# The five slots of the weight ring begin at five different distances from the moving tiles

## The chip, the cores and the metric

The kernel runs on one core of a Trainium2 chip. The metric is the device time of one execution in microseconds. Three runs of the kernel before took 790.16, 791.92 and 792.40 us; the median is 791.92 us.

## The reference, cut to what matters

One layer of a hybrid encoder block over 512 tokens of width 1024: a token mixer, a cross-attention into 256 memory tokens, and a SwiGLU feed-forward. All of it is float32. The change touches the feed-forward alone:

```python
def swiglu(h, w_gate_up, w_down):
    g, u = jnp.split(h @ w_gate_up, 2, axis=-1)
    return (jax.nn.silu(g) * u) @ w_down
...
        h = rms_norm(x, g_ffn_pre[l])
        x = x + rms_norm(swiglu(h, w_gate_up[l], w_down[l]), g_ffn_post[l])
```

`w_gate_up` is 1024 x 5632, `w_down` is 2816 x 1024.

## The kernel before, in words

Each float32 product is made from three matmuls (`mm3`, lines 139 to 142): every operand is split into a rounded part `hi` and a rest `lo`, and hi*hi, hi*lo and lo*hi are added up in PSUM. Line 140 loads the stationary hi and streams the moving hi, line 141 loads the same stationary hi again and streams the moving lo, line 142 loads the stationary lo and streams the moving hi. So every matmul has a weight load of 128 x 128 of its own, which runs beside the matmul before it: while TensorE streams one moving tile out of SBUF, it also reads the next stationary tile out of SBUF.

The gate and up projections after the first block run in units. Most units (`seven`, line 1077) use a Strassen-like scheme: 7 products of 12 matmuls with 256 columns each instead of 8. A few (`eight`, line 1040; blocks 2, 3 and 11) make all 8. There are 17 seven-units and 3 eight-units. The moving operands are the normalised activations `b1`, `b2` and sums of them, `thi` and `tlo`. The stationary operand is always a weight block out of a ring.

The ring is a pair of tiles, `ring_hi` and `ring_lo`, of 4160 float32 elements per partition (lines 869 and 870). Five slots stand in it: two single ones of 512 elements (one product each) and three double ones of 1024 elements (two products each, or half an eight-unit). `single()` and `double()` give the place at which a slot begins, in elements of 4 bytes, each in turn. A seven-unit takes one single slot and three double ones, an eight-unit two double ones. A slot is filled by a DMA into `raw`, for some of them sums on VectorE (lines 929 to 932), a cast on ScalarE into `ring_hi` (line 902) and a subtraction on VectorE into `ring_lo` (line 903). `take` fills a slot as soon as the items that overlap its place have been taken for use.

The compiled program puts `b1`, `b2`, the `t` tiles, `ring_hi` and `ring_lo` at addresses that are multiples of 256 bytes, and all steps inside them (256 or 128 elements) are multiples of 512 bytes. So the distance from the moving operand to the stationary one, modulo 256 bytes, is that of the slot alone. Before, `AS_WEIGHTS` is 16 elements: every slot begins at 64 bytes modulo 256.

After the gate and up blocks, the same ring holds `w_down` in four slots at 0, 1024, 2048 and 3072 elements (line 953). There the ring is the moving operand, in tiles of 512 columns. These four places stay as they are, and each overlaps the same old slots before and after.

Earlier stages hold other distances. In the first projection (lines 291 to 300) `hTh` and `hTl` are stationary, at multiples of 512 bytes, and `vhi`, `vlo` are moving. For the tile of 256 columns the distance is 0. For the tile of 264 columns block k begins at k times 1056 bytes, so the distance of stationary from moving is 192 bytes for k = 2, 160 for k = 3, 128 for k = 4, 96 for k = 5 and 64 for k = 6.

Of the kernel before, what the change touches and what calls it, by code (L numbers as in the profile page):

```python
# [32 lines left out]
AS_WEIGHTS, AS_MOVING = 16, 48  # L33
# [3 lines left out]
def hybrid_block_kernel(  # L37
# [606 lines left out]
    with tc.tile_pool(name="cross", bufs=1, reuse_waits="tile") as cp:  # L644
# [221 lines left out]

        ring_hi = cp.tile([P, 4160], F32R, tag="kT", name="ring_hi")
        ring_lo = cp.tile([P, 4160], F32R, tag="hh", name="ring_lo")  # L870
        sums = big.tile([P, 2, 4, 4, P], F32, tag="sB", name="sums")
# [36 lines left out]
        nslot = [0, 0]  # L908

        def single():  # L910
            nslot[0] += 1
            return AS_WEIGHTS + 512 * (nslot[0] % 2)

        def double():
            nslot[1] += 1
            return AS_WEIGHTS + 1024 + 1024 * (nslot[1] % 3)

        def seven_weights(n, c0):
            raw, total = {}, sums[:, n % 2]
            s2, s4, s3, s1 = (total[:, i] for i in range(4))  # L920

            def a11():
                raw["lower"] = load_raw(w_gate_up, 0, 4, c0, 256)
                raw["upper"] = load_raw(w_gate_up, 4, 4, c0, 256)
                return raw["lower"][:, :, :P]

            def s2_s4():
                lower, upper = raw["lower"], raw["upper"]
                dve.tensor_tensor(out=s1, in0=lower[:, :, P:], in1=upper[:, :, P:], op=ALU.add)
                dve.tensor_tensor(out=s2, in0=s1, in1=lower[:, :, :P], op=ALU.add)  # L930
                dve.tensor_tensor(out=s4, in0=s2, in1=upper[:, :, :P], op=ALU.add)
                dve.tensor_tensor(out=s3, in0=lower[:, :, :P], in1=lower[:, :, P:], op=ALU.add)
                return total[:, 0:2]

            two = dict(c=2, k=4, n=P)
            item(at := single(), 512, fill_from(at, dict(k=4, n=P), a11))
            item(at := double(), 1024, fill_from(at, two, s2_s4))
            item(at := double(), 1024, fill_from(at, two, lambda: raw["upper"], "p c k n -> p k c n"))
            item(at := double(), 1024, fill_from(at, two, lambda: total[:, 2:4]))
# [301 lines left out]
```

## Time and profile before

| | |
|---|---|
| median of three runs | 791.92 us |
| profiled execution, whole | 792.46 us |
| its span, first to last instruction | 790.4 us |
| TensorE busy | 766.5 us, 97% of the span, 4796 matmuls |
| VectorE, ScalarE busy | 554.4 us (70%), 413.6 us (52%) |
| ring stage with 256-column matmuls | about 464 to 663 us of the span |
| `w_down` stage | about 663 to 785 us |

The span is one execution as the profiler saw it; some 2.1 us of the time lie outside it. TensorE's busy time is nearly the span because a matmul counts as busy from its start to its modelled end, so matmuls overlap. How fast TensorE goes is therefore read from the starts: the time from one matmul's start to the next one's, or the number of matmuls in a stretch.

### The profile page before, as it was taken

The numbers are of one execution on the slowest core, as the hardware profiler recorded it, in microseconds if no ns is written. First come the engines' busy times: TensorE is split into PE (matmuls) and PEld (weight loads), VectorE is DVE, ScalarE is ACT, GpSimd is POOL, SyncE is SP. The second block draws the span as 40 slices with busy tenths as digits, with TensorE's granted clock in tenths as the row PEclk, the third lists the DMA queues.
The fourth block names the chain that finished last, engine by engine and source line by source line (L and its number), as shares of the span: only waits on it lengthen the run. The fifth ranks groups of instructions, "written<-read, shape, count | busy, mean of one in ns | idle before, by whom it ended". The sixth has DMA issues, their size and how long they took to land.

```text
span 790.4 us, 12322 instructions
## 1 busy us (share of the span) xinstructions
PE 766.5 (97%) x4796; PEld 674.0 (85%) x4796; DVE 554.4 (70%) x999; ACT 413.6 (52%) x755; POOL 70.6 (9%) x110
## 2 busy tenths in 40 slices
PE   7999999999999999999999999999999999999996
PEld 7887788887778888877778999999999999888885
DVE  6567889879886588545653778998899988414214
ACT  7358888757875457444543635544354448113111
POOL 6001232010321101000002100000000000000001
PEclk9999999999999999999999999999999999999998
DMA  6342112421322725411350212232433333423302
GB/s 243 84 130 57 52 55 75 138 72 64 107 80 96 282 77 187 131 56 54 134 160 0 81 49 86 81 108 82 148 99 107 103 107 114 152 80 107 106 2 107
DMA packets 60745, 80.01 MB, mean 101 GB/s; under 512 B 2704, under 2 KB 43664, under 8 KB 60688
## 3 DMA queue, kind: packets, MB, share of 16 engines
q1 hardware_dynamic: 59264, 74.49, 29.1%
q0 software_dynamic: 1280, 4.72, 1.8%
q8 instruction: 38, 0.62, 0.3%
q14 instruction: 19, 0.16, 0.1%
q10 hardware_dynamic: 144, 0.02, 0.0%
HBM read 77.13 MB, written 2.10 MB: 100 GB/s over the span
## 4 chain that ended last, share of the span: by engine, by line
PE 72%; DVE 11%; ACT 7%; issue 4%; DMA 3%; POOL 2%; SPq 0%; DVEq 0%; POOLq 0%; ACTq 0%
PE ps_a L141 14%; PE ps_a L140 14%; PE ps_a L142 14%; PE ps_s L140 4%; PE ps_s L142 4%; PE ps_s L141 4%; DVE ring_lo L903 3%; PE ps_t L140 2%; PE ps_t L141 2%; PE ps_t L534 2%; PE ps_t L142 2%; DMA raw<-in_dram 2%; PE ps_o L543 1%; PE ps_s L515 1%; PE ps_o L140 1%
## 5 line engine op out<-in xcount | busy, mean ns | idle before, releaser
L902 ACT CAST ring_hi<-fraw 128x1024 fp32r<-128x1024 f32 (+1 forms) x62 | 57.6, 933 | 102.6 <-PE ps_o L142 37.0
L903 DVE TENSOR_TENSOR ring_lo<-fraw,ring_hi 128x1024 fp32r<-128x1024 f32 (+1 forms) x62 | 66.6, 1076 | 63.2 <-ACT ring_hi L902 63.0
L126 DVE TENSOR_TENSOR lo<-raw,hi 128x1024 fp32r<-128x1024 f32 x56 | 68.2, 1224 | 22.2 <-ACT hi L125 21.9
L142 PE MATMUL ps_a<-hTh,lo 128*128 128x512 f32 x192 | 76.8, 400 | 0.6 <-DVE lo L126 0.6
L141 PE MATMUL ps_a<-hTl,hi 128*128 128x512 f32 x192 | 76.0, 396 | 0.0
L140 PE MATMUL ps_a<-hTh,hi 128*128 128x512 f32 x192 | 75.8, 395 | 0.2 <-ACT hi L125 0.2
L125 ACT CAST hi<-raw 128x1024 fp32r<-128x1024 f32 x56 | 57.8, 1048 | 24.4 <-PE ps_a L141 15.4
L902 ACT CAST ring_hi<-sums 128x1024 fp32r<-128x1024 f32 x34 | 35.7, 1050 | 56.5 <-PE ps_a L141 23.9
L903 DVE TENSOR_TENSOR ring_lo<-sums,ring_hi 128x1024 fp32r<-128x1024 f32 x34 | 41.5, 1222 | 4.3 <-ACT ring_hi L902 4.1
L142 PEld LDWEIGHTS ps_a<-hTh,lo 128*128 128x128 f32 x192 | 36.1, 188 | 7.3 <-DVE lo L126 1.0
L141 PEld LDWEIGHTS ps_a<-hTl,hi 128*128 128x128 f32 x192 | 36.1, 188 | 6.4
L140 PEld LDWEIGHTS ps_a<-hTh,hi 128*128 128x128 f32 x192 | 36.2, 188 | 6.1 <-ACT hi L125 0.4
L529 ACT ACTIVATE p<-p,nm 128x128 f32<-128x128 f32 (+1 forms) x64 | 36.1, 564 | 8.4 <-DVE nm L519 7.6
L140 PE MATMUL ps_a<-b,ring_hi 128*128 128x256 f32 x140 | 39.0, 279 | 0.0
L141 PE MATMUL ps_a<-b,ring_hi 128*128 128x256 f32 x140 | 39.0, 278 | 0.0
L142 PE MATMUL ps_a<-b,ring_lo 128*128 128x256 f32 x140 | 39.0, 278 | 0.0
L140 PE MATMUL ps_s<-b,ring_hi 128*128 128x256 f32 x128 | 35.5, 278 | 0.0
L141 PE MATMUL ps_s<-b,ring_hi 128*128 128x256 f32 x128 | 35.5, 278 | 0.0
L142 PE MATMUL ps_s<-b,ring_lo 128*128 128x256 f32 x128 | 35.5, 278 | 0.0
L536 ACT CAST pth<-ps_t 128x128 fp32r<-128x128 f32 (+1 forms) x64 | 27.1, 425 | 14.5 <-PE ps_t L534 13.7
L537 DVE TENSOR_TENSOR ptl<-ps_t,pth 128x128 fp32r<-128x128 f32 (+1 forms) x64 | 30.7, 487 | 4.9 <-ACT pth L536 3.6
L534 PE MATMUL ps_t<-ident,p 128*128 128x128 f32 x160 | 28.1, 275 | 1.1 <-DVE p L531 0.8
(425 smaller groups left out, 2504.4 us busy)
## 6 DMA issues: line engine op xcount, KB each, us to landing
raw<-in_dram SPq DMA_DIRECT2D x64, 512.0 KB, 3.6
fraw<-in_dram SPq DMA_DIRECT2D x62, 512.0 KB, 3.5
cb<-in_dram SPq DMA_DIRECT2D x8, 256.0 KB, 2.6
xo<-in_dram POOLq DMA_DIRECT2D x4, 512.0 KB, 5.6
out_dram<-yd SPq DMA_DIRECT2D x8, 256.0 KB, 2.0
rawv<-in_dram SPq DMA_DIRECT2D x3, 520.0 KB, 6.1
xt<-in_dram SPq DMA_DIRECT2D x3, 512.0 KB, 6.9
gb<-in_dram POOLq DMA_DIRECT2D x3, 512.0 KB, 5.1
```

The costliest lines, as they stand in the source:

```text
L125: act.copy(hi[:, j : j + n, :], raw)
L126: dve.tensor_tensor(out=lo[:, j : j + n, :], in0=raw, in1=f32(hi[:, j : j + n, :]), op=ALU.subtract)
L140: pe.matmul(dst, sh, mh, start=first, stop=False)
L141: pe.matmul(dst, sh, ml, start=False, stop=False)
L142: pe.matmul(dst, sl, mh, start=False, stop=last)
L515: pe.matmul(s[:, :w], q[:, h, ts], kt[:, h, :w], start=True, stop=False)
L529: act.activation(p[:, :n], p[:, :n], AF.Exp, bias=nm, scale=-1.0, accum_out=sm)
L534: pe.transpose(tp[:, k * P : (k + 1) * P], p[:, k * P : (k + 1) * P], ident)
L536: act.copy(span(ph, i), t3)
L537: dve.tensor_tensor(out=span(pl, i), in0=t3, in1=f32(span(ph, i)), op=ALU.subtract)
L902: act.copy(h2, v)
L903: dve.tensor_tensor(out=l2, in0=v, in1=f32(h2), op=ALU.subtract)
```

## The change

Only the five places change, as multiples of 4 bytes: the two single slots begin at 16 and 536 elements (64 and 96 bytes modulo 256) in place of 16 and 528; the three double ones at 1056, 2088 and 3120 (128, 160 and 192 bytes) in place of 1040, 2064 and 3088. No instruction is added or removed and none is moved; the order on every queue stays.

```diff
         def single():
             nslot[0] += 1
-            return AS_WEIGHTS + 512 * (nslot[0] % 2)
+            return (16, 512 + 24)[nslot[0] % 2]
 
         def double():
             nslot[1] += 1
-            return AS_WEIGHTS + 1024 + 1024 * (nslot[1] % 3)
+            return (1024 + 32, 2048 + 40, 3072 + 48)[nslot[1] % 3]
```

(A blank line is added ahead of line 869, so later lines of the kernel after stand one further down.)

## Rows read from the trace of the kernel before

**Rows 1.** The page: span, busy time, and the span in 40 slices.
```profile
span 790.4 us, 12322 instructions
...
PE 766.5 (97%) x4796; PEld 674.0 (85%) x4796; DVE 554.4 (70%) x999; ACT 413.6 (52%) x755; POOL 70.6 (9%) x110
...
PE   7999999999999999999999999999999999999996
...
PEclk9999999999999999999999999999999999999998
```

**Rows 2.** Busy time by stretch, all engines (us and instructions; clock, DMA share, GB/s).
```profile
core 0: us, PE busy (x) PEld busy (x) DVE busy (x) ACT busy (x) POOL busy (x), PEclk, DMA share, GB/s
454.00:493.00 39.00, 39.00 (x334) 39.00 (x333) 32.54 (x38) 17.15 (x21) 0.00 (x0) 1.00 0.19 59
493.00:603.00 110.00, 107.77 (x939) 106.78 (x939) 101.65 (x146) 52.40 (x79) 0.00 (x0) 1.00 0.35 109
603.00:634.00 31.00, 31.00 (x260) 30.58 (x259) 30.22 (x45) 13.64 (x21) 0.00 (x0) 1.00 0.33 105
634.00:663.00 29.00, 28.61 (x252) 28.42 (x251) 23.73 (x34) 15.85 (x27) 0.00 (x0) 1.00 0.27 92
663.00:785.00 122.00, 121.03 (x540) 100.11 (x538) 44.32 (x57) 30.78 (x44) 2.21 (x4) 1.00 0.27 95
```

**Rows 3.** Matmuls alone, in stretches without a pause.
```profile
core 0: us, PE busy (x), PEclk, DMA share, GB/s
464.00:493.00 29.00, 29.00 (x249) 1.00 0.20 62
555.00:583.00 28.00, 28.00 (x250) 1.00 0.41 127
604.00:613.00 9.00, 9.00 (x79) 1.00 0.30 90
614.00:633.00 19.00, 19.00 (x164) 1.00 0.31 97
634.00:643.00 9.00, 9.00 (x82) 1.00 0.31 105
644.00:662.00 18.00, 18.00 (x161) 1.00 0.25 88
686.00:718.00 32.00, 32.00 (x143) 1.00 0.22 78
```

**Rows 4.** Timeline of TensorE around 607 us, first and thirteenth matmul.
```profile
606.20 0.28 PE L140 MATMUL ps_a<-thi,ring_hi 128*128 128x256 f32 x1
...
607.62 0.28 PE L140 MATMUL ps_a<-b,ring_hi 128*128 128x256 f32 x1
```

**Rows 5.** Timeline of TensorE around 566 us, first and tenth matmul.
```profile
565.87 0.28 PE L140 MATMUL ps_a<-b,ring_hi 128*128 128x256 f32 x1
...
566.89 0.28 PE L140 MATMUL ps_a<-b,ring_hi 128*128 128x256 f32 x1
```

**Rows 6.** What TensorE waited for, 486 to 663 us (total, times, longest).
```profile
PE ps_t L140 <- DVE U L1090: 1.7, 2, 1.3
PE ps_a L140 <- DVE G L1090: 0.8, 3, 0.4
```

**Rows 7.** Timeline, first projection, 256 columns at distance 0, first and twelfth.
```profile
21.40 0.28 PE L140 MATMUL ps_a<-vhi,hTh 128*128 128x256 f32 x1
...
22.72 0.28 PE L142 MATMUL ps_a<-vhi,hTl 128*128 128x256 f32 x1
```

**Rows 8.** Timeline, first projection, 264 columns, first and last for k = 2 to 6.
```profile
12.51 0.28 PE L140 MATMUL ps_s<-vhi,hTh 128*128 128x264 f32 x1
...
13.59 0.28 PE L140 MATMUL ps_a<-vhi,hTh 128*128 128x256 f32 x1
...
15.03 0.28 PE L140 MATMUL ps_s<-vhi,hTh 128*128 128x264 f32 x1
...
16.49 0.28 PE L140 MATMUL ps_a<-vhi,hTh 128*128 128x256 f32 x1
...
20.29 0.29 PE L140 MATMUL ps_s<-vhi,hTh 128*128 128x264 f32 x1
...
21.28 0.29 PE L142 MATMUL ps_o<-vhi,hTl 128*128 128x264 f32 x1
...
22.84 0.29 PE L140 MATMUL ps_s<-vhi,hTh 128*128 128x264 f32 x1
...
24.30 0.28 PE L140 MATMUL ps_a<-vhi,hTh 128*128 128x256 f32 x1
...
29.18 0.29 PE L142 MATMUL ps_s<-vhi,hTl 128*128 128x264 f32 x1
...
30.03 0.28 PE L140 MATMUL ps_a<-vhi,hTh 128*128 128x256 f32 x1
```

**Rows 9.** Instructions that write `ring_hi` and `ring_lo`: ns min/median/max, first and last start.
```profile
L902 ACT CAST ring_hi<-fraw x62: 609/1048/1057, 436.7 to 762.3; 128x1024 fp32r<-128x1024 f32 x45, 128x512 fp32r<-128x512 f32 x17
L903 DVE TENSOR_TENSOR ring_lo<-fraw,ring_hi x62: 683/1220/1228, 437.9 to 763.4; 128x1024 fp32r<-128x1024 f32 x45, 128x512 fp32r<-128x512 f32 x17
```

## The prediction

> **What bounds the kernel now.** First the page: TensorE is busy for 766.5 of 790.4 us and its granted clock stands at 9 tenths or more in every slice but the last [rows 1]. So the end moves by what TensorE's pace moves, wherever TensorE does not wait. Then the stretches: the change acts only where the ring is stationary, about 464 to 663 us. There VectorE is the nearest other engine, 101.65 of 110 us between 493 and 603 us, and 30.22 of 31 us between 603 and 634 us; ScalarE is at half [rows 2]. TensorE's idle time from 493 to 603 us is 110 - 107.77 = 2.2 us, and the waits put it on VectorE's sums of the seven-units: 1.7 us before a product into `ps_t`, 0.8 us before one into `ps_a` [rows 2, 6].
>
> The view that matters is the pace of the matmuls, by count. A matmul lasts 0.28 us and is counted in every window it touches, so the time per matmul is (window + 0.28) / count. It has two values in the ring stage: 28.28 / 250 = 113.1 ns from 555 to 583 us, and 29.28 / 249 = 117.6 ns from 464 to 493 us [rows 3]. The starts say the same: 1.02 us over nine steps, 113.3 ns, around 566 us; 1.42 us over twelve steps, 118.3 ns, around 607 us [rows 4, 5]. I use 113.3 and 117.7. From 634 to 643 us it is 113.2, from 644 to 662 us 113.5, from 604 to 613 us 117.5, from 614 to 633 us 117.6 [rows 3]. So a stretch is wholly fast or wholly slow, and the pace changes at TensorE's pauses, not with the slot, the moving tile or the load of the other engines: the granted clock is 1.00 in both. This looks like two read streams, moving tile and next weights, that fall into step after a pause and stay so, since every matmul repeats the same distance of 64 bytes. This lock is my reading; the rows show the two paces and that they last.
>
> How much is lost to it: the slow stretches run from about 463.7 to 493.3 and from 603.4 to 633.3 us, less some 0.6 us of pauses, so (29.6 + 29.3) us / 117.7 ns = 500 matmuls at 4.4 ns over the fast pace: 2.2 us. All the ring's 256-column matmuls are 17 x 84 + 3 x 96 = 1716 by the code, so 29% are slow.
>
> **The change part by part.** Nothing is added, removed or moved on any queue; no wait is new. Three things could cost or give.
>
> (a) The writes into the ring start at other offsets. The casts and subtractions of `fraw` run both at 64 bytes modulo 256 (gate and up) and at 0 (`w_down`), and the longest is 9 and 8 ns over the median of 1048 and 1220 ns [rows 9]. 17 x 4 + 3 x 2 = 74 slots are filled; 74 x 8 ns = 0.6 us on VectorE is an end upward, as much downward the other. No row has an odd multiple of 32 bytes for these. I take 0; ScalarE, half idle, covers its share, and VectorE's would lie beside TensorE except in the 2.2 us of waits.
>
> (b) The pace at the new distances. Of the 1716 matmuls, 204 use single slots (half stay at 64 bytes, half go to 96) and 1512 use double ones, 504 each at 128, 160 and 192. No row shows 256 columns at these. Bounds: the fast end is 113.3 ns, because the `w_down` stage, where a 512-column matmul gives the weights twice the time, goes at 32.39 us / 143 = 226.5 ns, the same per column [rows 3]; the stream itself seems to need that. The slow end is distance 0 with 256 columns, 1.32 us / 11 = 120.0 ns [rows 7]. All 1512 at 120.0 cost 10.1 us against all fast, 7.9 us more than the 2.2 us lost today; all fast gains 2.2 us.
>
> Between these ends stand the 264-column rows of the first projection, the only ones at the new distances [rows 8]: at 192 bytes 1.08 us / 9 = 120.0 ns, at 160 1.46 / 12 = 121.7, at 128 0.99 / 8 = 123.8, at 96 1.46 / 12 = 121.7, and at 64 0.85 / 7 = 121.4. These are no prices for 256 columns (at 64 bytes the ring itself has 113.3 or 117.7), so I use only their differences from 64 bytes: +2.4 ns at 128, +0.3 at 160, -1.4 at 192, +0.3 at 96. 504 x (2.4 + 0.3 - 1.4) ns + 102 x 0.3 ns = +0.7 us. Each stretch there has about ten matmuls, so this sum is hardly different from 0; I take 0 and keep the 0.7 for the range.
>
> (c) The lock. A slot is left after 12, 24 or 48 matmuls, and the next one stands at another distance, so the streams are shifted against each other by 32 bytes or more. If each slot then draws anew at today's odds, 29% stay slow, only better mixed: no gain. If a fast stretch survives the shift and a slow one ends with its slot, nearly all 2.2 us come back. No row shows a shift without a pause, so I take the middle, 1.1 us. What is late next is VectorE: in the slow stretch from 603 to 634 us it is busy for 30.22 of 31 us, so at most 0.8 us can be won there [rows 2]; half of that stretch's 1.1 us fits, and none of the gain is hidden.
>
> **Sum.** Profiled execution 792.46 (span 790.4 and 2.1 outside) + 0 + 0 - 1.1 = 791.4 us. That is 0.5 under the median of 791.92; the three runs, 790.16 to 792.40, are just as far apart as the 2.2 us between all fast and today's mix.
>
> At two places the Trainium skill says otherwise. The rows show a pace that differs between distance 0 (120.0 ns) and 64 (113.3 or 117.7) [rows 3, 7]. The page "SBUF — State Buffer", section "Who interferes with whom", gives TensorE two independent read ports for moving operand and weights, and says that TensorE never waits on anyone; by that rule distances would not matter and the time would stay at 792.46 us. The trace speaks against it. And the page "TensorE: Matmul & The Clock Gate", section "Back-to-back issue gap", gives N / 2.4 + 2.5 ns, 109.2 ns for 256 columns, as the gap; no stretch of the ring gets there.
>
> **The rivals.**
>
> *Slower: the new distances lock worse.* The 128-byte slots fall to the pace of distance 0 and the other double ones to the slow pace. For it: 128 bytes is the slowest of the 264-column rows, and no double slot keeps the 64 bytes that have the fast pace [rows 8]. Against: 192 bytes is the fastest of them. Price: 504 x 6.7 + 1008 x 4.4 = 7.8 us, less today's 2.2 = 5.6; TensorE's 2.2 us of waits on VectorE can swallow part, since there a slower TensorE waits less: 3.4 to 5.6, so 795.9 to 798.1 us. It decides from 545 more slow matmuls than today's 500 (2.4 us).
>
> *The change does nothing.* Whatever sets the pace at a pause, hardware other than the distance, holds on through the slots: 792.46 us, or whatever mix of stretches the run draws, 790.2 to 792.5. For it: paces change only at pauses today. Against: distance 0 differs from 64.
>
> *Faster: a third pace.* At some distance the streams never meet, and the matmul goes below 113.3 ns. For a price I take the same step downward as from slow to fast, 4.4 ns, for two of the three double slots: 1008 x 4.4 + 2.2 = 6.6 us, 785.8 us, with VectorE's 92% [rows 2] giving back up to half: 785.8 to 789. Against: 226.5 ns at 512 columns says that 113.3 is the stream's own.
>
> **How the numbers follow.** Less than 0.3%, 2.4 us, can't be told from no change in this kernel. The forecast (locks end sooner; from 790.2, all fast, to 793.2, no gain and the 0.7 of (b)) has 0.50; nothing changes 0.15; locks worse 0.26; a third pace 0.09. The all-fast end of the forecast, 790.2, is within 0.3% of the median, so faster holds the third pace and a little of the forecast: 0.13. Slower is the worse lock and its milder mixes: 0.28. Same is 0.59. The range from 789.3 to 796.6 leaves out most of the third pace and the upper half of the worse lock.
>
> **What would show it.** Right: in the profile after, no stretch of 20 us in the ring stage stands at 117.7 ns throughout; the count per stretch lies between the two paces, and the pace changes at slots. Wrong: one slot with its own pace of 118 ns or more in every unit (worse lock), the paces still changing only at pauses (nothing), or any stretch under 113 ns (third pace). The casts and subtractions into the ring should keep 1048 and 1220 ns; if they lengthen, (a) was mis-sized. What would overturn the forecast most cheaply is the 128-byte slot at 120 ns: 504 x 6.7 = 3.4 us by itself.

## The result, and the profile after

The kernel after takes 794.93 us (median of 20 runs, 793.47 to 796.46), the kernel before 791.86 us (20 runs, 789.21 to 794.77). The ratio is 1.0044, 95% interval 1.0035 to 1.0053: slower by 0.44%. The forecast was 791.4.

The page of the kernel after, its span, busy time and slices, against [rows 1]:

```profile
span 792.6 us, 12322 instructions
...
PE 772.3 (97%) x4796; PEld 680.9 (86%) x4796; DVE 554.1 (70%) x999; ACT 413.3 (52%) x755; POOL 71.5 (9%) x110
...
PE   8999999999999999999999999999999999999996
...
PEclk9999999999999999999999999999999999999998
```

Same instructions, same granted clock; TensorE is busy 5.8 us longer, and the span grew by 2.2. Busy time by stretch, all engines, against [rows 2] (the last stretch begins 2.5 us later, since the ring stage ends later):

```profile
core 0: us, PE busy (x) PEld busy (x) DVE busy (x) ACT busy (x) POOL busy (x), PEclk, DMA share, GB/s
454.00:493.00 39.00, 38.97 (x331) 38.76 (x331) 32.59 (x38) 17.38 (x21) 0.00 (x0) 1.00 0.22 68
493.00:603.00 110.00, 109.30 (x919) 108.56 (x918) 99.64 (x142) 50.85 (x76) 0.00 (x0) 1.00 0.32 102
603.00:634.00 31.00, 30.94 (x264) 30.73 (x264) 30.08 (x44) 13.71 (x20) 0.00 (x0) 1.00 0.33 104
634.00:665.50 31.50, 31.45 (x266) 31.24 (x266) 25.95 (x38) 17.37 (x29) 0.00 (x0) 1.00 0.30 100
665.50:785.00 119.50, 119.50 (x533) 99.16 (x533) 43.33 (x54) 29.34 (x42) 2.21 (x4) 1.00 0.26 93
```

Between 493 and 603 us 919 matmuls stand where 939 stood, although TensorE is idle for 0.7 us in place of 2.2. So each matmul takes longer. The waits of TensorE from 486 to 667 us are down to one, against 1.7 and 0.8 us [rows 6]:

```profile
PE ps_t L140 <- DVE U L1091: 0.6, 1, 0.6
```

Matmuls alone, in stretches without a pause of note, against [rows 3]:

```profile
core 0: us, PE busy (x), PEclk, DMA share, GB/s
464.00:492.00 28.00, 28.00 (x238) 1.00 0.22 66
497.00:511.00 14.00, 14.00 (x120) 1.00 0.23 75
555.00:583.00 28.00, 28.00 (x240) 1.00 0.37 116
636.00:664.00 28.00, 28.00 (x239) 1.00 0.28 95
686.00:718.00 32.00, 32.00 (x143) 1.00 0.24 82
```

With the same reckoning, (window + 0.28) / count: 118.8, 119.0, 117.8 and 118.3 ns in the ring stage. None of these stretches is at 113.3 any more. The `w_down` stage, which the change leaves alone, has the same 143 matmuls in 32 us.

The pace is now that of the slot. The starts of the first matmul of three double slots in a row, 48 matmuls each (blocks 2 and 3, made in full), and of the single slot behind them; then those of two later double slots, 24 apart:

```profile
466.87 0.28 PE L140 MATMUL ps_a<-b,ring_hi 128*128 128x256 f32 x1
...
472.53 0.28 PE L140 MATMUL ps_s<-b,ring_hi 128*128 128x256 f32 x1
...
478.23 0.28 PE L140 MATMUL ps_s<-b,ring_hi 128*128 128x256 f32 x1
...
483.98 0.28 PE L140 MATMUL ps_a<-b,ring_hi 128*128 128x256 f32 x1
...
570.86 0.28 PE L140 MATMUL ps_a<-b,ring_hi 128*128 128x256 f32 x1
...
573.58 0.28 PE L140 MATMUL ps_a<-tlo,ring_hi 128*128 128x256 f32 x1
```

The slot at 192 bytes: 5.66 us / 48 = 117.9 ns. The one at 128: 5.70 / 48 = 118.8. The one at 160: 5.75 / 48 = 119.8. The 192-byte slot again at 570.86: 2.72 / 24 = 113.3. So 192 has the two paces that 64 had, and 128 and 160 are slow each in its own way: in every unit the 128-byte slot took 118.3 to 119.0 ns a step and the 160-byte slot 119.2 to 120.1.

Over the whole ring stage, from all starts in the trace, each slot's mean time from one start to the next (steps over 130 ns, the pauses, left out; before, where all slots stand at 64 bytes, the mean of all):

| slot, distance | matmuls | before, ns | after, ns | added, us |
|---|---|---|---|---|
| single, 64 bytes | 96 | 114.7 | 115.6 | 0.1 |
| single, 96 | 108 | 114.7 | 118.3 | 0.4 |
| double, 128 | 504 | 114.7 | 118.6 | 2.0 |
| double, 160 | 504 | 114.7 | 119.8 | 2.6 |
| double, 192 | 504 | 114.7 | 116.3 | 0.8 |

That is 5.8 us (column added: matmuls times the difference). The time above 113.3 ns in the steps over 130 ns shrank from 4.95 to 2.72 us, so 2.2 us of it went into waits that TensorE had anyway. Left are 3.5 us; the ring stage, from its first to its last matmul (13 early ones, done between those of the first block, left out), grew from 200.20 to 203.61 us, 3.4 us. In the two profiled executions the stages ahead of the ring happened to take 1.2 us less after (463.9 and 462.7 us to its first matmul), which gives the 2.2 us of the spans. The medians are 3.1 us apart.

The writes into the ring kept their durations, against [rows 9]:

```profile
L903 ACT CAST ring_hi<-fraw x62: 611/1048/1057, 435.8 to 764.6; 128x1024 fp32r<-128x1024 f32 x45, 128x512 fp32r<-128x512 f32 x17
L904 DVE TENSOR_TENSOR ring_lo<-fraw,ring_hi x62: 683/1219/1228, 437.0 to 765.6; 128x1024 fp32r<-128x1024 f32 x45, 128x512 fp32r<-128x512 f32 x17
```

### The profile page after: what moved, and what is told of

It reads as the page before. It is cut to its first block, busy times and chain, and to the rows that moved or that the text cites. A ratio compares the mean times of both kernels' runs of the same rounds, so it can differ in the third digit from the quotient of the medians.

```text
span 792.6 us, 12322 instructions
## 1 busy us (share of the span) xinstructions
PE 772.3 (97%) x4796; PEld 680.9 (86%) x4796; DVE 554.1 (70%) x999; ACT 413.3 (52%) x755; POOL 71.5 (9%) x110
## 4 chain that ended last, share of the span: by engine, by line
PE 75%; DVE 9%; ACT 6%; issue 4%; DMA 3%; POOL 2%; SPq 0%; DVEq 0%; POOLq 0%; ACTq 0%
PE ps_a L140 14%; PE ps_a L141 14%; PE ps_a L142 14%; PE ps_s L141 4%; PE ps_s L142 4%; PE ps_s L140 4%; PE ps_t L140 2%; PE ps_t L141 2%; PE ps_t L142 2%; DVE ring_lo L904 2%; PE ps_t L534 2%; DMA raw<-in_dram 2%; PE ps_o L543 1%; PE ps_o L140 1%; PE ps_o L141 1%
```

## The experiments

Three explanations stood against each other. A: each distance between the moving tile and the next weights has paces of its own, and 96, 128 and 160 have bad ones. B: it is the shift at each slot change that costs. C: the offset of a slot by itself is bad, whatever the place of the moving tile. All kernels are the one before with other places in the ring; the diffs show the two lines of `single()` and `double()`.

**All slots at 128.**

```diff
-            return AS_WEIGHTS + 512 * (nslot[0] % 2)
+            return (32, 512 + 32)[nslot[0] % 2]
...
-            return AS_WEIGHTS + 1024 + 1024 * (nslot[1] % 3)
+            return (1024 + 32, 2048 + 32, 3072 + 32)[nslot[1] % 3]
```

> All five slots at 128 bytes modulo 256, so no slot change shifts the distance. Theory A (each distance has its own pace; 128 is one of the bad ones): every ring stretch at 118 to 119 ns per matmul, as in the 128-byte slot of the changed kernel; 1716 x (118.6 - 114.7) = 6.7 us more than before, less 2 to 4 us that the waits on VectorE swallow: 794.5 to 797 us. Theory B (it is the shift at each slot change that costs, whatever the distance): no shifts, so the two paces of before, 113.3 and 117.7 ns, and 790 to 793 us.

Measured 795.07 us (8 runs), ratio 1.0043 [1.0027, 1.0058] to the kernel before.

**All slots at 160.** The same with 40 in place of 32.

> All five slots at 160 bytes modulo 256. Theory A: 119.8 to 120.4 ns throughout, 1716 x 5.3 = 9 us, less 3 to 5 us of waits on VectorE that shrink: 796 to 798.5 us, slower than with all at 128. Theory B: no shifts, 790 to 793 us.

Measured 796.47 us (6 runs), ratio 1.0057 [1.0040, 1.0073].

**All slots at 192.** The same with 48.

> All five slots at 192 bytes modulo 256, which in the changed kernel ran partly at 113.3 and partly at 117.7 ns. Theory A: the same two paces as at 64 bytes, changing at pauses, and 790 to 794 us. Theory B: also as before, 790 to 793 us. A third possibility: 192 was fast only where a 160-byte slot came before it; then it stays at 117.7 throughout, 1716 x 3 = 5 us less waits, 793.5 to 795.5 us.

Measured 793.39 us (12 runs), ratio 1.0014 [1.0002, 1.0026]. The same three stretches of each of these kernels follow, with columns as above; the count of matmuls is the number to read. All slots at 128:

```profile
464.00:484.00 20.00, 20.00 (x171) 1.00 0.26 76
544.00:564.00 20.00, 20.00 (x171) 1.00 0.36 107
647.00:663.00 16.00, 16.00 (x137) 1.00 0.27 92
```

All slots at 160:

```profile
464.00:484.00 20.00, 20.00 (x169) 1.00 0.26 78
544.00:564.00 20.00, 20.00 (x169) 1.00 0.34 106
647.00:663.00 16.00, 16.00 (x136) 1.00 0.23 69
```

All slots at 192:

```profile
464.00:484.00 20.00, 20.00 (x179) 1.00 0.24 66
544.00:564.00 20.00, 20.00 (x172) 1.00 0.41 122
647.00:663.00 16.00, 16.00 (x138) 1.00 0.21 67
```

At 128: 20.28 / 171 = 118.6 ns, then 118.6 and 118.8. At 160: 20.28 / 169 = 120.0, then 120.0 and 119.7. At 192: 113.3 in the first stretch, 117.9 and 118.0 in the others, the two paces of 64 bytes. With no shift at all, 128 and 160 are as slow as in the changed kernel. B as the whole cause is out; A holds. 192 was at its slow pace for most of that profile (15% of the steps at 113 or 114 ns, against 69% with all at 64), and its median lies 1.5 us over the kernel before.

**64 and 192 in turn: a miss of mine.**

```diff
+            return (16, 512 + 48)[nslot[0] % 2]
...
+            return (1024 + 16, 2048 + 48, 3072 + 16)[nslot[1] % 3]
```

> The two distances that have a fast pace, in turn (singles 64 and 192, doubles 64, 192, 64): as many shifts as in the changed kernel, by 128 bytes each. Theory A: only 113.3 and 117.7 ns are seen, 790 to 793.5 us. Theory B (shifts cost): paces of 118 and more after every slot change, 793.5 to 796 us. If a shift ends a slow stretch, as I forecast, the slow share falls under that of before and the time is 790 to 791 us.

Measured 808.89 us (5 runs), ratio 1.0207 [1.0188, 1.0225]. The second single slot now ends at 512 + 48 + 512 = 1072 elements and the first double one begins at 1040; the third double begins 32 elements inside the second. Slots that overlap can't be filled while the neighbour is in use. What TensorE waited for from 480 to 680 us:

```profile
PE ps_a L142 <- DVE ring_lo L903: 3.8, 7, 1.3
PE ps_s L140 <- ACT ring_hi L902: 2.8, 3, 1.1
PE ps_s L142 <- DVE ring_lo L903: 2.7, 5, 0.8
```

It waits for the ring itself, which neither kernel does. Between the waits most steps were at 113.3 or 117.7 ns, at both distances. The time tells nothing of A or B.

**64 and 192 without overlap.**

```diff
+            return (16, 512 + 16)[nslot[0] % 2]
...
+            return (1024 + 16, 2048 + 48, 3072 + 48)[nslot[1] % 3]
```

> Again 64 and 192 bytes in one ring, this time with slots that don't overlap: singles and the first double slot at 64, the other two doubles at 192, so two shifts in a seven-unit. It is the changed kernel with its three bad distances (96, 128, 160) taken out. Theory A (each distance has its own paces): only 113.3 and 117.7 ns, 790 to 793.5 us, so about 2 us or more below the changed kernel's 794.9. Theory B (shifts cost by themselves): 118 ns and more after each shift, 793.5 to 796 us. My forecast's idea that a shift ends a slow stretch: the pace turns to 113.3 within a slot or two of each pause, 790 to 791 us.

Measured 791.62 us (12 runs), ratio 1.0004 [0.9991, 1.0016]: level with the kernel before, so these shifts by 128 bytes cost nothing that the runs can tell. Only the two paces appear. And here the forecast's own mechanism can be seen. The starts around a change from a 192-byte slot to a 64-byte one (at 601.78 us):

```profile
597.54 0.28 PE L140 MATMUL ps_t<-b,ring_hi 128*128 128x256 f32 x1
...
601.78 0.28 PE L140 MATMUL ps_s<-tlo,ring_hi 128*128 128x256 f32 x1
601.90 0.28 PE L141 MATMUL ps_s<-tlo,ring_hi 128*128 128x256 f32 x1
602.01 0.28 PE L142 MATMUL ps_s<-tlo,ring_lo 128*128 128x256 f32 x1
602.12 0.28 PE L140 MATMUL ps_s<-tlo,ring_hi 128*128 128x256 f32 x1
```

36 steps in 4.24 us ahead of it, 117.8 ns; then 0.34 us for three, 113.3, and from 601.8 to 612.5 us 10.98 / 97 = 113.2. Over the whole ring stage a slow stretch met this change ten times and ended there, or within the next six matmuls, eight times. The change the other way, from 64 to 192, ended none of the four slow stretches that met it, so it isn't the shift as such that frees one. Yet the time did not fall. In this profile the steps took 114.5 ns on average against 114.7 before, but each pause can start a slow stretch anew, and the waits for VectorE grew: from 486 to 667 us 3.1 us against the 2.5 us of before [rows 6]:

```profile
PE ps_a L140 <- DVE G L1090: 1.6, 5, 0.4
PE ps_t L140 <- DVE U L1090: 1.5, 2, 1.4
```

**Ten other distances, in two kernels.** Singles at 0 and 32 bytes, doubles at 80, 208 and 224; then singles at 16 and 48, doubles at 112, 176 and 240.

```diff
+            return (0, 512 + 8)[nslot[0] % 2]
...
+            return (1024 + 20, 2048 + 52, 3072 + 56)[nslot[1] % 3]
```

```diff
+            return (4, 512 + 12)[nslot[0] % 2]
...
+            return (1024 + 28, 2048 + 44, 3072 + 60)[nslot[1] % 3]
```

> One look for the paces by slot: singles at 0 and 32 bytes, doubles at 80, 208 and 224. Theory A: 0 at 120 as in the first projection; 32 and 224 like 96 and 160 (118 to 120), being odd multiples of 32; 80 and 208, 16 bytes past 64 and 192, between 113.3 and 120. Any slot that stands at 113.3 in every unit would be the distance to use.

> One look for the paces by slot: singles at 16 and 48 bytes, doubles at 112, 176 and 240. Theory A: each has a settled pace of its own between 113.3 and 120; no rows yet tell which. A slot always at 113.3 would be the one to use.

One run each, 793.36 and 794.22 us. The mean steps in ns, as in the table above (those of the other runs added, each marked with *):

| distance | 0 | 16 | 32 | 48 | 64* | 80 | 96* | 112 | 128* | 160* | 176 | 192* | 208 | 224 | 240 |
|---|---|---|---|---|---|---|---|---|---|---|---|---|---|---|---|
| mean step | 119.2 | 118.2 | 118.5 | 118.0 | 113.3 or 117.7 | 118.8 | 118.3 | 119.8 | 118.7 | 120.0 | 118.2 | 113.3 or 117.7 | 116.8 | 116.8 | 119.2 |

No distance tried is always at 113.3, and only 64 and 192 held it through whole slots. A slot of 12 to 48 matmuls includes the first few steps after a change, so the means of the probed ones are a little off their settled pace. A mean can also hide two paces: at 240 bytes the slot of 24 matmuls that began at 504.57 us took 2.81 us, 117.1 ns each, and the one at 514.76 us 2.87 us, 119.6; five of the nineteen slots at 240 were of the faster kind. My guess for 32 and 224 (118 to 120) held for 32 alone.

**Moving tile shifted under the same slots.** All slots at 128, and the moving sums `thi` and `tlo` begin at 64 bytes:

```diff
-            wp.tile([P, 2, 4, 256], F32R, tag=tag, name=f"t{tag}", bufs=2) for tag in ("hi", "hi", "lo", "lo")
+            wp.tile([P, KB * 256 + 48], F32R, tag=tag, name=f"t{tag}", bufs=2)[:, 16 : 16 + 2048].rearrange(
+                "p (s k n) -> p s k n", s=2, k=4
+            )
+            for tag in ("hi", "hi", "lo", "lo")
```

> All five slots at 128 bytes as in the first experiment, but the moving sums (thi and tlo, 4 of the 7 products of a seven-unit) begin at 64 bytes in place of 0; b1 and b2 stay at 0. So the same slots are read at distance 64 under the sums and at 128 under b1 and b2. Theory A (the distance between moving and stationary counts): products with the sums at 113.3 or 117.7 ns once settled, products with b1 and b2 at 118 to 119; 816 matmuls some 3 ns faster than with all at 128, 2.4 us less before the waits on VectorE: 793 to 795 us. Rival C (the slot's own offset counts, 128 bytes being bad to read or write from): both at 118 to 119 ns, and 795 us as with all at 128.

Measured 794.06 us (6 runs), ratio 1.0038 [1.0021, 1.0055]. From the fourth matmul of a slot's product with `thi` on, then the next two products, with `b2` out of the same slot and with `b1` out of the next one:

```profile
546.01 0.28 PE L140 MATMUL ps_a<-thi,ring_hi 128*128 128x256 f32 x1
...
547.03 0.28 PE L140 MATMUL ps_a<-b,ring_hi 128*128 128x256 f32 x1
...
549.88 0.28 PE L140 MATMUL ps_o<-tlo,ring_hi 128*128 128x256 f32 x1
```

Nine steps with `thi` in 1.02 us, 113.3 ns; 24 with `b1` and `b2` in 2.85, 118.8. Over the stage the sums' products took 116.6 ns a step (both paces), the others 118.7, out of the same slots. So the place of a slot by itself doesn't set the pace: C is out. The time alone would not say so, since it fits what was expected under C as well. The distance between the two operands fits all the runs here. One rival to it stays untested: that 64 bytes is a good place for the moving tile whatever the slot. No run reads a ring slot at 64 with the moving tile there, which would be distance 0.

**The changed kernel without its 160-byte slot.**

```diff
+            return (16, 512 + 24)[nslot[0] % 2]
...
+            return (1024 + 32, 2048 + 48, 3072 + 48)[nslot[1] % 3]
```

> The changed kernel with one slot put back to a good distance: singles at 64 and 96, doubles at 128, 192, 192 in place of 128, 160, 192. Theory A: no pace of 119 to 120 ns is left; 504 x (119.8 - 116.3) = 1.8 us less than the changed kernel before waits, so 793 to 794.3 us, still 1 to 2 us over the kernel before because of the 128-byte slot and 192 at its slow pace. Theory B (shifts cost): nearly as many shifts, so 794.5 to 795.5 us.

Measured 793.58 us (9 runs), ratio 1.0030 [1.0019, 1.0040]: by the ratios about 1.1 us of the 3.5 came back (the two intervals just overlap), where the expectation's sum was 1.8 before waits. Steps: 118.5 ns at 128, 115.7 at 192, 118.3 at 96.

## Why the prediction was wrong

**The bound was read rightly.** TensorE's pace sets the ring stage, and a change of it came through to the end, less what the waits on VectorE took: 5.8 us by steps, 3.4 us in the stage.

**(a) held.** The writes cost nothing at odd multiples of 32 bytes.

**(b) failed; this is the step.** "This sum is hardly different from 0; I take 0." The steps grew by 5.8 us, whatever (c) gave back included. I had the right bounds, 113.3 and 120.0 ns, and then let the 264-column rows [rows 8] choose inside them. They rank the distances wrongly: 128 as the worst, 160 no worse than 64; in the ring 160 is the worst (120.0), 128 second (118.7). A matmul of 264 columns ends 32 bytes further on modulo 256 than it began, so it may never settle in the state that 256 columns repeat; that is a guess, and no run tests it. I had written that these rows are no prices, and used their differences as prices all the same. The nearest row in kind, 256 columns at distance 0 [rows 7], pointed the right way: a settled distance other than 64 can lose 6.7 ns on each matmul, and only 64 had a fast row.

**(c) was half right as a mechanism and worth nothing here.** A shift can end a slow stretch, but not any shift: the change from 192 to 64 did so eight times in ten, the one from 64 to 192 in none of four. In the changed kernel three of the five slots have no fast pace to fall into. And with the two good distances alone the time stayed level: in that profile the steps saved 0.5 us and the pauses took 0.8 us more. I had counted on no loss to VectorE, because the slow stretches of that one profile lay where TensorE had little idle time.

**The rivals.** "The new distances lock worse" is what happened, and its sign came: slots with a pace of 118 ns or more in every unit, those at 128 and 160. Its sum, 7.8 - 2.2 us less 2.2 of waits, gave 3.4 us for the stage, just the measured growth. That is partly luck: 128 and 160 are exchanged in it, and 192 is put at its slow pace throughout, where it was at its fast one in 7 of 19 slots. "The change does nothing" fell with the paces by slot, and no distance of fifteen gave a third pace under 113.3 ns for a whole slot. The Trainium skill ("SBUF — State Buffer", section "Who interferes with whom") calls TensorE's read ports for the moving operand and for the weights independent. The prediction took from this that distances would not matter; here they did, by up to 6.7 ns of 120. Whether TensorE ever waits on another engine's reads or writes, which the same section denies, no run here shows.

What stays open: why some distances, 64, 192 and 240 among them, have more than one pace, and why 113.3 ns lasted at 64 and 192 only. The experiments show that the pace hangs on the places of both operands, and at 64 and 192 on what came before; what inside the chip makes it so, no run here shows.

## What to carry to other kernels

When weights are loaded beside a stream of matmuls, look at the time from start to start, not at busy time, and treat the distance between stationary and moving tile as a size to measure: one run with several distances in several slots tells the bad ones from the rest. For a distance with two paces it shows only those that this run fell into: 192 was fast in 7 of its 19 slots in the changed kernel and slow for 85% of the steps when all slots stood there. Rows of another shape give bounds for such a size, not a ranking. Ask first what the stage's second engine would take back: here all slots in the fast pace are worth (114.7 - 113.3) ns x 1,716 matmuls = 2.4 us of 792, and VectorE takes part of that.

## What was not expected of the hardware

With all slots at one distance modulo 256 bytes, a matmul of 256 columns with its own weight load took 118.7 ns on average at 128 bytes, 120.0 at 160, and 113.3 or 117.7 at 64 and 192, with the granted clock at 1.00 in all. Of these last two states each can last for hundreds of matmuls. It changed only at a pause or a shift, and not every pause changes it: with all slots at 192 the slow one held from about 492 us to the end of the ring stage. The 512-column matmuls of `w_down` kept their 226.5 ns in both kernels.
